# Spreading the gates into G in one pipeline of fixed order, with a tile of scores beside every 16 tokens and 52 tiles ahead

## The chip, the core and the metric

The kernel runs on one core of a Trainium2 chip. The metric is the device time in microseconds (us); the kernel before takes 2368.05 us, the median of 3 runs. TensorE (PE) does the matrix products, VectorE (DVE) and ScalarE (ACT) the elementwise work, GpSimd (POOL) some elementwise work and the issue of indirect DMAs, SyncE (SP) the issue of all other DMAs.

## The reference, cut to what matters

The program is two transformer blocks. The change lies in the feed-forward of the first, a mixture of 16384 experts (`u` and `v` are [16384, 1024]) of which each of 512 tokens uses 16 for each of 8 heads:

```python
def block(xi):
    q = (xi @ w_q).reshape(n, 8, 2, 128)
    s = jnp.einsum('nhpc,hpkc->nhpk', q, sub_keys)
    ts, ti = lax.top_k(s, 16)
    cand_s = ts[:, :, 0, :, None] + ts[:, :, 1, None, :]       # 16 x 16 pairs
    cand_i = ti[:, :, 0, :, None] * 128 + ti[:, :, 1, None, :]
    best_s, best_p = lax.top_k(cand_s, 16)
    idx = jnp.take_along_axis(cand_i, best_p, axis=-1)
    gate = jax.nn.softmax(best_s, axis=-1)
    act = gelu(jnp.einsum('nd,nhkd->nhk', xi, u[idx]))
    return jnp.einsum('nhk,nhkd->nd', gate * act, v[idx])
```

## The kernel before

For the first 384 tokens the kernel computes every expert: G[expert, token] holds the gates, zero where an expert is not chosen, and the result is the sum over 128 tiles of 128 experts of v_tile^T (G * gelu(u_tile x)). For the last 128 tokens it gathers the 128 chosen rows of u and of v for each token.

Products are made in three passes (`mm3`, lines 220 to 223): high half by high half, and the two mixed ones. A tile of u (512 KB) is split on the chip: `wsplit` loads it (`uraw`), ACT makes the high half `uhi` (line 233), and VectorE or POOL makes the low half `ulo` (line 234). `prep_u(i)` does this for tile i; `upass(i)` makes its 24 matmuls of 384 columns into `pu` and its gelu `ge` on ACT (line 986). `prep_u` gives the low half to POOL for tiles 3 to 41 and to VectorE for the others.

The stage runs in this order:

- **Routing** (16 column tiles of w_q): PE makes queries and scores, VectorE the sorted choices. After each column tile, `ahead` computes one or two tiles of u x ahead of time, 24 in all; their gelus go to DRAM (`sd`).
- **Spread**: G for 384 tokens. `spread(nt)` takes 128 tokens. It transposes the two key numbers and the gates (line 1096), makes doubled copies (`tw`), and then for every 64 tokens the short one-hot rows `bh`, `eql`, `bl` (lines 1114 to 1120). For every 8 tokens VectorE makes three operands of 128 x 1024 in 16 bits: the one-hot `oa` (line 1125) and two products `ob` (line 1131). PE multiplies them, 16 matmuls of 128 columns for 8 tokens (line 1139), into two PSUM tiles `pq`, and ACT copies each of these to `gs` or `gk` (line 1140), from where 64 tokens at a time go to DRAM (`gd`). Every fourth group of 8 tokens `ahead(1)` adds a tile of u x, 12 in all; `ahead(NG)` then does the rest up to NG = 43. The order of all this on the engines is set by a scheduler with priorities and modelled times.
- **Loop** over 128 tiles of v. `prep_v(i)` loads a tile of v and of G (`gt`), gets the scores (`gl` from DRAM for i < NG, `ge` from `upass` otherwise), multiplies them with G on VectorE (lines 1185, 1186), and splits both (`vhi`, `vlo`, `ch`, `cl`); `vpass(i)` makes 18 matmuls of 512 columns into `po`. From tile 43 on, `upass(i + 1)` runs beside `vpass(i)`. VectorE's order is written out by hand.
- The loop also holds the 256 gathers (128 of u rows, then 128 of v rows; `gr`, three buffers, 512 KB each). POOL issues them (line 1206), VectorE consumes them in order (line 1211 for u, line 1220 for v), between the low half of a tile of u and the products with G. Their number in one turn of the loop follows from a cost of 2 for a turn with a tile of u and 0.5 for one without: with NG = 43 the total is 187.5, which makes 256 x 2 / 187.5 = 2.73 gathers in a turn with u, and 0.68 in one without.

Of the kernel before, what the change touches and what calls it, by code (L numbers as in the profile page):

```python
# [20 lines left out]
D = 1024  # L21
# [10 lines left out]
# the even tokens, and the odd ones  # L32
# [133 lines left out]
def _nabias(rpb):  # L166
    """[4 blocks, 8 heads, 128 queries (c, r), 256 keys (c, r)]: the bias, or NEG outside the window"""
# [14 lines left out]
def _sib():  # L182
    """pairs (j, i) whose blocks of s are siblings, s = 1..32"""
    j = np.arange(128)[:, None]
    i = np.arange(128)[None, :]
    return np.stack([(((j // s) ^ (i // s)) == 1).astype(np.float32) for s in (1, 2, 4, 8, 16, 32)], 1)


def program(tc, a, dbg=None):
# [54 lines left out]
    def rstd_of(pool, ps, n, feat, eps, tag="rs", bufs=1, b=None):  # L244
        """-2 feat / sqrt(ps / feat + eps), with one Newton step; the gains carry the factor -1 / (2 feat)"""
# [10 lines left out]
    def warm_rs(after):  # L256
        """the table of the norms, ahead of one"""
# [6 lines left out]
    # ---------------------------------------------------------------- first block, mixing  # L264
# [11 lines left out]
    NG = 43  # L276
    GT = 3
    GN = 3
    OAN = 8
    PQB = 6  # L280
    # the order of the first projection's parts; the last one runs after the others' pools are closed
# [20 lines left out]
    with ExitStack() as es:  # L302
# [10 lines left out]
        def ada_steps():  # L313
            """the conditioning columns: products of rows of the transposed weights with the vectors, and their sums"""
# [29 lines left out]
        def weights():  # L344
            """the next tile of weights; the ones after it are on their way"""
# [14 lines left out]
        # the norm's factor scales the products' columns; the operands hold the gains alone  # L360
# [26 lines left out]
        def rs_columns():  # L387
            """the factor of a token's row, for tiles that have the tokens on the partitions"""
# [14 lines left out]
        def rotate(raw, j):  # L403
            """rotary embedding of a projected tile"""
# [103 lines left out]
        for o in order[:NT]:  # L508
            if o == 'z':
                x0.close()  # L510
                zp = x0.enter_context(tc.tile_pool(name="z", bufs=1, reuse_waits="tile"))
                # lambda
# [8 lines left out]
                V.tensor_scalar(lam, lam, 0.8 - 0.6, -1.0, op0=OP.add, op1=OP.mult)   # -lambda  # L521
# [14 lines left out]
        # ------------------------------------------------ gated linear attention, both directions  # L536
# [12 lines left out]
        def gla_pair(hp):  # L549
# [9 lines left out]
            def diag(h):  # L559
                """the 128 x 128 blocks on the diagonal of A^T"""  # L560
# [79 lines left out]
            # the meta tokens: forward, from the end of their decay to the start of the sequence  # L640
# [42 lines left out]
    # ------------------------------------------------ conditioning of the second block  # L683
# [6 lines left out]
    scl = const.tile([128, 3, KT], F32, name="scl")   # norm gain * (1 + scale): latent 1, context, latent 2  # L690
# [48 lines left out]
        # ------------------------------------------------ differential attention  # L739
# [123 lines left out]
    def shifted(pool, src, n, sc_, sh, rs, hi, lo):  # L863
        """src * gain * rs + shift in two halves"""
# [21 lines left out]
    with ExitStack() as es:  # L886
# [5 lines left out]
        # the context: its norm now, its keys and values behind the output projection  # L892
# [54 lines left out]
    # ------------------------------------------------ experts: scores and routes  # L947
# [20 lines left out]
    # ------------------------------------------------ experts: every expert for the first 384 tokens  # L968
# [10 lines left out]
    def upass(i):  # L979
        wh, wl = us.pop(i)  # L980
        p = psU.tile([128, ND], F32, name="pu")
        for k in range(KT):
            w_ = (wh[:, k * 128:k * 128 + 128], wl[:, k * 128:k * 128 + 128])
            mm3(p, w_, (hn[0][:, k, :ND], hn[1][:, k, :ND]), k == 0, k == KT - 1)
        ge = up.tile([128, ND], F32, name="ge", bufs=4)
# [6 lines left out]
    with ExitStack() as es:  # L992
# [7 lines left out]
        def route(h):  # L1000
            """the 16 best pairs of a head, as two key numbers, for every token"""
            tf = wp.tile([128, 4, 2, 16], BF16, name="tf")
            V.tensor_copy(tf, ti[:, :, 2 * h:2 * h + 2])
            # a pair (a, b) of ranks can be among the best 16 only if (a + 1) (b + 1) <= 16
# [28 lines left out]
            for c in range(2):  # L1033
                # the best 8 have ranks below 8
# [35 lines left out]
        # gates: a softmax over the 16 of each head, the first of which is the largest  # L1070
# [6 lines left out]
    # the last 64 tokens' part stays on chip  # L1077
# [13 lines left out]
    def spread(nt):  # L1091
        """G[i2, i1, n], through DRAM: a sum of products of one-hot rows, the gates scaled and in two halves"""
# [4 lines left out]
        # i1 = 16 a + b; every number twice, so that the last step of an operand is one element  # L1097
        iu = rp.tile([128, 2, 128], U32, name="iu", bufs=1)
        V.tensor_copy(iu[:, 0], p[:, 0:128])
        V.tensor_scalar(iu[:, 1], iu[:, 0], 15, None, op0=OP.bitwise_and)  # L1100
        tw = [rp.tile([128, 128, 2], F16, name=f"tw{j}", bufs=1) for j in range(5)]
        d2 = [128, 128, 2]
        V.tensor_copy(tw[1], iu[:, 1, :, None].to_broadcast(d2))
        V.tensor_tensor(tw[0], p[:, 0:128, None].to_broadcast(d2), tw[1], op=OP.subtract)
        S.copy(tw[2], p[:, 128:256, None].to_broadcast(d2))
        S.mul(tw[3], p[:, 256:384, None].to_broadcast(d2), GS)
        V.scalar_tensor_tensor(tw[4], p[:, 256:384, None].to_broadcast(d2), GS, tw[3], op0=OP.mult, op1=OP.subtract)
        for n0 in range(0, 128, 64):
            tb = nt * 2 + n0 // 64
            gs = gk if tb % 2 else rp.tile([128, 128, 64], F32, name="gs")  # L1110
            ns = slice(n0, n0 + 64)
            bh = rp.tile([128, 64, 8, 2], F16, name="bh", bufs=1)
            eq = rp.tile([128, 64, 16], F16, name="eql", bufs=1)
            V.tensor_tensor(bh, iotah[:, None].to_broadcast([128, 64, 8, 2]),
                            tw[0][:, ns, None, :].to_broadcast([128, 64, 8, 2]), op=OP.is_equal)
            V.tensor_tensor(pairs(eq), pairs(iota16[:, None, 0:16]).to_broadcast([128, 64, 8, 2]),
                            tw[1][:, ns, None, :].to_broadcast([128, 64, 8, 2]), op=OP.is_equal)
            bl = rp.tile([128, 2, 64, 16], F16, name="bl", bufs=1)
# [680 lines left out]
```

## Time and profile before

| | |
|---|---|
| time, median of 3 runs (lowest to highest) | 2368.05 us (2366.97 to 2370.98) |
| the profiled execution: span from first to last instruction | 2382.4 us |
| PE, weight loads, VectorE, ACT, POOL busy in it | 95%, 80%, 72%, 42%, 30% |
| start of the spread, start of the loop's first matmul | about 638 us, 805.86 us |
| turn of the loop without u, with u | about 4.07 us, 8.35 us |

The page of the profile gives no other time of the profiled execution than its span; it is 14.35 us (0.6%) above the median of the runs without a profile, so differences in it are carried over to the median as they are. Matmuls are pipelined, and the record of one reaches into the next, so the rate of the PE is read from the distances of starts or the number of matmuls in a stretch, not from busy time. [...]

### The profile page before, as it was taken

The numbers are of one execution on the slowest core, as the hardware profiler recorded it, in microseconds if no ns is written. First come the engines' busy times: TensorE is split into PE (matmuls) and PEld (weight loads), VectorE is DVE, ScalarE is ACT, GpSimd is POOL, SyncE is SP. The second block draws the span as 40 slices with busy tenths as digits, with TensorE's granted clock in tenths as the row PEclk, the third lists the DMA queues.
The fourth block names the chain that finished last, engine by engine and source line by source line (L and its number), as shares of the span: only waits on it lengthen the run. The fifth ranks groups of instructions, "written<-read, shape, count | busy, mean of one in ns | idle before, by whom it ended". The sixth has DMA issues, their size and how long they took to land.

```text
span 2382.4 us, 30940 instructions
## 1 busy us (share of the span) xinstructions
PE 2258.9 (95%) x11457; PEld 1895.9 (80%) x11457; DVE 1722.6 (72%) x3152; ACT 993.4 (42%) x1439; POOL 703.3 (30%) x428
## 2 busy tenths in 40 slices
PE   7999898999888999999999999999998999999997
PEld 6876466899767888899999987889877677788885
DVE  8997776799988677777777767778679565433334
ACT  5337774333277533333333323333443654322322
POOL 2132213344333311234343444443463023000001
PEclk9999998999989999999999999999999999999999
DMA  7760022533255899889999888889521221322320
GB/s 252 254 212 9 1 102 76 183 124 102 98 194 229 323 307 305 292 312 327 313 315 326 293 279 286 293 296 339 173 98 53 69 93 50 136 98 89 106 89 36
DMA packets 153831, 448.69 MB, mean 188 GB/s; under 512 B 14768, under 2 KB 58160, under 8 KB 151888
## 3 DMA queue, kind: packets, MB, share of 16 engines
q1 hardware_dynamic: 116768, 312.36, 37.5%
q0 software_dynamic: 36912, 134.37, 16.4%
q8 instruction: 89, 1.46, 0.2%
q14 instruction: 62, 0.51, 0.1%
HBM read 415.15 MB, written 31.52 MB: 187 GB/s over the span
## 4 chain that ended last, share of the span: by engine, by line
PE 73%; DVE 12%; DMA 6%; issue 4%; ACT 3%; POOL 2%; DVEq 0%; POOLq 0%; SPq 0%; ACTq 0%
PE pu L223 6%; PE pu L221 6%; PE po L221 6%; PE po L222 6%; PE po L223 6%; PE pu L222 6%; DMA gr<-in_v,idx 5%; PE psB L221 3%; PE psB L222 2%; PE psB L223 2%; PE pm L222 2%; PE pm L223 2%; PE pm L221 2%; PE pa L221 2%; PE pa L222 2%
## 5 line engine op out<-in xcount | busy, mean ns | idle before, releaser
L223 PE MATMUL pu<-hn,ulo 128*128 128x384 f32 x1024 | 353.4, 345 | 12.5 <-POOL ulo L234 12.5
L221 PE MATMUL pu<-hn,uhi 128*128 128x384 f32 x1024 | 354.2, 346 | 0.8 <-ACT uhi L233 0.8
L222 PE MATMUL pu<-hn,uhi 128*128 128x384 f32 x1024 | 351.7, 343 | 0.0
L221 PE MATMUL po<-vhi,ch 128*128 128x512 f32 x768 | 302.8, 394 | 9.4 <-ACT ch L1187 9.4
L222 PE MATMUL po<-vlo,ch 128*128 128x512 f32 x768 | 302.3, 394 | 0.4
L223 PE MATMUL po<-vhi,cl 128*128 128x512 f32 x768 | 300.8, 392 | 0.0
L234 POOL TENSOR_TENSOR wlo<-wraw,whi 128x1024 fp32r<-128x1024 f32 x57 | 144.5, 2540 | 398.0 <-ACT whi L233 328.2
L233 ACT CAST whi<-wraw 128x1024 fp32r<-128x1024 f32 x109 | 114.0, 1049 | 345.0 <-PE pm L222 126.7
L1206 POOL DMA_INDIRECT gr<-in_u,idx x128 | 148.2, 1158 | 344.8 <-DVE aact L1211 324.8
L1206 POOL DMA_INDIRECT gr<-in_v,idx x128 | 177.4, 1386 | 231.9 <-DVE acc L1220 190.7
L233 ACT CAST uhi<-uraw 128x1024 fp32r<-128x1024 f32 x129 | 135.6, 1051 | 248.9 <-PE pu L222 215.0
L1220 DVE SCALAR_TENSOR_TENSOR acc<-gr,aact,acc 128x1024 f32<-128x1024 f32 x126 | 159.0, 1280 | 87.7 <-DMA gr<-in_v,idx 87.1
L223 PEld LDWEIGHTS pu<-hn,ulo 128*128 128x128 f32 x1024 | 194.9, 190 | 13.4 <-POOL ulo L234 13.1
L221 PEld LDWEIGHTS pu<-hn,uhi 128*128 128x128 f32 x1024 | 194.9, 190 | 4.9 <-ACT uhi L233 0.9
L222 PEld LDWEIGHTS pu<-hn,uhi 128*128 128x128 f32 x1024 | 194.5, 190 | 4.1
L1176 ACT CAST vhi<-vraw 128x1024 fp32r<-128x1024 f32 x128 | 134.4, 1050 | 149.5 <-PE po L223 92.0
L1188 DVE TENSOR_TENSOR vlo<-vraw,vhi 128x1024 fp32r<-128x1024 f32 x128 | 156.1, 1220 | 42.9 <-ACT vhi L1176 42.9
L234 DVE TENSOR_TENSOR wlo<-wraw,whi 128x1024 fp32r<-128x1024 f32 x52 | 63.5, 1222 | 160.7 <-ACT whi L233 160.6
L221 PEld LDWEIGHTS po<-vhi,ch 128*128 128x128 f32 x768 | 144.5, 188 | 40.9 <-ACT ch L1187 13.3
L1211 DVE CUSTOM_DVE_ANT_0 gr<-gr,hnat 128x1024 f32<-128x1024 f32 x128 | 153.7, 1220 | 27.8 <-DMA gr<-in_u,idx 27.5
L223 PEld LDWEIGHTS po<-vhi,cl 128*128 128x128 f32 x768 | 144.4, 188 | 35.1 <-DVE cl L1189 4.0
L234 POOL TENSOR_TENSOR ulo<-uraw,uhi 128x1024 fp32r<-128x1024 f32 x39 | 123.2, 3163 | 157.8 <-ACT uhi L233 149.0
(567 smaller groups left out, 5106.1 us busy)
## 6 DMA issues: line engine op xcount, KB each, us to landing
uraw<-in_ut SPq DMA_DIRECT2D x129, 512.0 KB, 5.1
vraw<-in_v SPq DMA_DIRECT2D x128, 512.0 KB, 5.6
aw<-in_ada SPq DMA_DIRECT2D x48, 512.0 KB, 4.9
gt<-gd SPq DMA_DIRECT2D x42, 480.0 KB, 7.3
wraw<-in_m SPq DMA_DIRECT2D x32, 512.0 KB, 3.7
xraw<-in_m SPq DMA_DIRECT2D x32, 512.0 KB, 4.2
gd<-gs SPq DMA_DIRECT2D x6, 2048.0 KB, 9.8
sd<-ge SPq DMA_DIRECT2D x43, 192.0 KB, 2.1
```

What stands on the lines that cost most here:

```text
L221: PE.matmul(out, lhs[0], rhs[0], start=first, stop=False)
L222: PE.matmul(out, lhs[0], rhs[1], start=False, stop=False)
L223: PE.matmul(out, lhs[1], rhs[0], start=False, stop=last)
L233: S.copy(hi, raw)
L234: eng.tensor_sub(lo, raw, hi.bitcast(F32))
L1176: S.copy(wh, raw)
L1188: V.tensor_sub(wl, raw, wh.bitcast(F32))
L1206: G.indirect_dma_start(r, None, src, bass.IndirectOffsetOnAxis(ap=idx[:, j:j + 1], axis=0))
L1211: V.tensor_tensor_reduce(out=r, in0=r, in1=hnat, scale=1.0, scalar=0.0, op0=OP.mult, op1=OP.add, accum_out=aact[:, j:j + 1])
L1220: V.scalar_tensor_tensor(A, r, aact[:, j:j + 1], A, op0=OP.mult, op1=OP.add)
```

## The change

- The spread is written as one pipeline of 48 steps of 8 tokens. VectorE, ACT and PE follow the order in which it is written (`manual_schedule`).
- Every two steps (16 tokens) one tile of u x runs: 24 tiles, 26 to 49. Within a step PE does 8 of the spread's matmuls, then 6 of the tile's, and both again.
- VectorE makes the operands of step s + 2 while PE works on step s; `oa` and `ob` have three buffers in place of two. The short rows are made for 32 tokens at a time, not 64.
- The low halves of these 24 tiles are made on VectorE; POOL makes them for tiles 3 to 26.
- The last tokens' index list (`idx`) is made at step 3, not ahead of the spread.
- NG is 52 in place of 43: 24 tiles in routing as before, 2 between routing and the spread, 24 in the spread, 2 behind it. The loop then has 52 turns without u, and the total of its costs is 174: 2.94 gathers in a turn with u, 0.74 in one without.

```diff
-    NG = 43
+    NR = 26
+    NG = 52
...
-            us[i] = wsplit(up, a['ut'][i], bufs=2, tag="u", eng=G if 3 <= i < NG - 1 else V)
+            us[i] = wsplit(up, a['ut'][i], bufs=2, tag="u", eng=G if 3 <= i <= NR else V)
+
+    def prep_u_hi(i):
+        raw = up.tile([128, 1024], F32, name="uraw", bufs=3)
+        nc.sync.dma_start(raw, a['ut'][i])
+        us[i] = [up.tile([128, 1024], F32R, name=t, bufs=2) for t in ("uhi", "ulo")] + [raw]
+        S.copy(us[i][0], raw)
+
+    def prep_u_lo(i):
+        hi, lo, raw = us[i]
+        V.tensor_sub(lo, raw, hi.bitcast(F32))
...
+    CH = 32
...
+    def spread_rows(t):
+        tw = tws[t // 128]
+        ns = slice(t % 128, t % 128 + CH)
...
+    def spread_ops(s):
+        if s * 8 % CH == 0:
+            spread_rows(s * 8)
...
+        oa = rp.tile([128, 8, 128], F16, name="oa", bufs=3)
...
+        ob = rp.tile([128, 2, 8, 128], F16, name="ob", bufs=3)
...
-    for nt in range(3):
-        for b, _ in enumerate(spread(nt)):
-            if b % 8 in (1, 5):
-                ahead(1)
...
-    ahead(NG)
+    NS = 48
+    with tc.manual_schedule(engines={e.engine for e in (nc.vector, nc.scalar, nc.tensor)}):
+        i0 = ges["next"]
+        for i in range(i0, NR):
+            prep_u(i + 1)
+            upass(i)
+        spread_pre(0)
+        spread_ops(0)
+        spread_ops(1)
+        ti = NR
+        held = None
+        for s in range(NS):
+            if s % 2 == 0:
+                if held is not None:
+                    ugelu(*held)
+                prep_u_hi(ti + 1)
+                held = ti, psU.tile([128, ND], F32, name="pu")
+            if s + 2 < NS:
+                spread_ops(s + 2)
+            if s % 2 == 0:
+                prep_u_lo(ti + 1)
+            if s % 16 == 12 and s < 32:
+                spread_pre(s // 16 + 1)
+            for q0 in (0, 4):
+                spread_mm(s, q0)
+                k0 = (s % 2) * 4 + q0 // 2
+                umm(*held, range(k0, k0 + 2))
+            if s % 2:
+                ti += 1
...
+        ugelu(*held)
+        for i in range(ti, NG):
+            prep_u(i + 1)
+            upass(i)
```

On VectorE in the spread, before: the end of one 8-token group, the short rows of the next 64 tokens, and the next `oa`.

```order
L1131 TENSOR_TENSOR ob<-bh,bl 128x1024 x2
L1116 TENSOR_TENSOR eql<-iota_5646,tw_5658 128x1024
L1114 TENSOR_TENSOR bh<-iotah,tw_5657 128x1024
L1120 TENSOR_TENSOR bl<-eql,tw_5660 128x1024
L1120 TENSOR_TENSOR bl<-eql,tw_5661 128x1024
L1125 TENSOR_TENSOR oa<-iota_5646,tw_5659 128x1024
```

The same place of VectorE in the changed kernel, where lines 1142 to 1162 make the same operands and line 971 the low half of a tile of u.

```order
L1142 TENSOR_TENSOR bh<-iotah,tw_6302 128x512
L1143 TENSOR_TENSOR eql<-iota_5646,tw_6303 128x512
L1146 TENSOR_TENSOR bl<-eql,tw_6305 128x512
L1146 TENSOR_TENSOR bl<-eql,tw_6306 128x512
L1157 TENSOR_TENSOR oa<-iota_5646,tw_6304 128x1024
L1162 TENSOR_TENSOR ob<-bh,bl 128x1024 x2
L971 TENSOR_TENSOR ulo<-uraw,uhi 128x1024
```

The short rows are half as long, and a low half stands in VectorE's row after every second group.

On POOL from the end of routing to the end of the gathers, before (`cw0lo` belongs to the second block).

```order
L234 TENSOR_TENSOR ulo<-uraw,uhi 128x1024 x20
L1206 DMA gr<-in_u,idx 128x1024 x2
L234 TENSOR_TENSOR ulo<-uraw,uhi 128x1024
L1206 DMA gr<-in_u,idx 128x1024 x126
L1206 DMA gr<-in_v,idx 128x1024 x128
```

The same place of POOL in the changed kernel.

```order
L234 TENSOR_TENSOR wlo<-wraw,whi 128x1024
L234 TENSOR_TENSOR ulo<-uraw,uhi 128x1024 x6
L1274 DMA gr<-in_u,idx 128x1024 x128
L1274 DMA gr<-in_v,idx 128x1024 x128
L234 TENSOR_TENSOR cw0lo<-uraw,cw0hi 128x1024
```

Of 21 low halves 6 are left on POOL, all ahead of the spread, and its next work is the gathers.

On VectorE in the loop, in the part with the gathers of v, before: the sums of gathered rows (`acc`) in one turn, then the products with G and the splits, and the next turn's low half.

```order
L234 TENSOR_TENSOR ulo<-uraw,uhi 128x1024
L1220 SCALAR_TENSOR_TENSOR acc_7622<-gr,aact,acc_7622 128x1024
L1220 SCALAR_TENSOR_TENSOR acc_7621<-gr,aact,acc_7621 128x1024
L1185 TENSOR_TENSOR ge<-ge,gt 128x320
L1186 TENSOR_TENSOR ge<-ge,gk 128x64
L1188 TENSOR_TENSOR vlo<-vraw,vhi 128x1024
L1189 TENSOR_TENSOR cl<-ge,ch 128x384
```

The same part of VectorE's row in the changed kernel.

```order
L234 TENSOR_TENSOR ulo<-uraw,uhi 128x1024
L1288 SCALAR_TENSOR_TENSOR acc_7973<-gr,aact,acc_7973 128x1024
L1288 SCALAR_TENSOR_TENSOR acc_7972<-gr,aact,acc_7972 128x1024
L1288 SCALAR_TENSOR_TENSOR acc_7973<-gr,aact,acc_7973 128x1024
L1253 TENSOR_TENSOR ge<-ge,gt 128x320
L1254 TENSOR_TENSOR ge<-ge,gk 128x64
L1256 TENSOR_TENSOR vlo<-vraw,vhi 128x1024
L1257 TENSOR_TENSOR cl<-ge,ch 128x384
```

Before, a turn with two gathers follows every two or three turns with three; now turns with three follow each other up to 21 times.

## Rows read from the trace of the kernel before

**Rows 1.** Windows by stage: length, engines' busy time (instructions), granted clock, DMA share, GB/s.

```profile
638.00:806.00 168.00, 140.27 (x1199) 122.63 (x1200) 130.29 (x201) 117.08 (x139) 67.66 (x18) 0.89 0.57 216
806.00:977.00 171.00, 171.00 (x755) 141.28 (x754) 127.27 (x225) 63.08 (x86) 25.56 (x27) 1.00 0.93 313
977.00:1290.00 313.00, 313.00 (x1575) 285.48 (x1575) 244.37 (x390) 112.40 (x150) 122.68 (x101) 1.00 0.90 315
1290.00:1700.00 410.00, 400.14 (x1955) 354.56 (x1955) 310.62 (x362) 134.52 (x186) 174.55 (x126) 1.00 0.85 297
```

**Rows 2.** Waits of PE from 420 to 810 us: total us, times, longest.

```profile
PE pq L1139 <- DVE ob L1131: 15.0, 5, 4.8
PE pu L223 <- POOL ulo L234: 12.5, 3, 4.7
```

**Rows 3.** Waits of VectorE: 977 to 1290 us (first two), 1290 to 1700 us.

```profile
DVE ge L1185 <- ACT ge L986: 40.2, 29, 3.4
DVE gr L1211 <- DMA gr<-in_u,idx: 27.5, 24, 3.4
DVE acc L1220 <- DMA gr<-in_v,idx: 87.1, 48, 7.0
DVE ge L1185 <- ACT ge L986: 10.7, 9, 2.5
```

**Rows 4.** The sums of v rows on VectorE: count, shortest/median/longest ns, first and last start.

```profile
L1220 DVE SCALAR_TENSOR_TENSOR acc<-gr,aact,acc x126: 1273/1280/1306, 1295.8 to 1695.5; 128x1024 f32<-128x1024 f32 x126
```

**Rows 5.** Gathers of v rows on POOL, 1290 to 1700 us: busy, mean ns | idle; landing.

```profile
L1206 POOL DMA_INDIRECT gr<-in_v,idx x126 | 175.6, 1393 | 230.6 <-DVE acc L1220 190.7 <-DMA gr<-in_v,idx 20.8 <-issue 14.3
DMA to landing us min/median/max: 4.0/6.1/11.6
```

**Rows 6.** Timeline of PE in the spread and at both its ends: start, length, what.

```profile
653.33 0.28 PE L1139 MATMUL pq<-ob,oa 128*128 128x128 f16 x2 [3.15 <-DVE ob L1131]
...
674.03 0.95 PE L1139 MATMUL pq<-ob,oa 128*128 128x128 f16 x14
674.79 0.42 PE L223 MATMUL pu<-hn,ulo 128*128 128x384 f32 x1
675.05 0.34 PE L221 MATMUL pu<-hn,uhi 128*128 128x384 f32 x1
...
805.86 0.39 PE L221 MATMUL po<-vhi,ch 128*128 128x512 f32 x1
```

**Rows 7.** Timeline of VectorE: end of routing, and groups of the spread.

```profile
640.78 0.67 DVE L1076 TENSOR_TENSOR gate<-gate,gz 128x512 f32<-128x512 f32 x1
...
669.58 0.68 DVE L1116 TENSOR_TENSOR eql<-iota,tw 128x1024 f16<-128x1024 f16 x1
...
671.98 0.68 DVE L1125 TENSOR_TENSOR oa<-iota,tw 128x1024 f16<-128x1024 f16 x1
...
673.79 0.68 DVE L1125 TENSOR_TENSOR oa<-iota,tw 128x1024 f16<-128x1024 f16 x1
```

**Rows 8.** Timeline of ACT in the spread.

```profile
674.63 3.84 ACT L1140 ACTIVATE gk<-pq 128x512 f32<-128x512 f32 x4 [0.93 <-PE pq L1139]
678.24 1.08 ACT L233 CAST uhi<-uraw 128x1024 fp32r<-128x1024 f32 x1
...
680.90 0.56 ACT L986 ACTIVATE ge<-pu 128x384 f32<-128x384 f32 x1
```

**Rows 9.** Low halves on POOL in the spread, and on VectorE in the loop.

```profile
671.53 14.09 POOL L234 TENSOR_TENSOR ulo<-uraw,uhi 128x1024 fp32r<-128x1024 f32 x2 [7.84 <-ACT uhi L233]
L234 DVE TENSOR_TENSOR ulo<-uraw,uhi 128x1024 fp32r<-128x1024 f32 x86 | 104.6, 1216 | 0.0
```

**Rows 10.** A window of 25 us in the loop, columns as in rows 1.

```profile
1625.00:1650.00 25.00, 25.00 (x127) 22.80 (x126) 21.59 (x27) 8.87 (x13) 9.18 (x9) 1.00 0.94 344
```

**Rows 11.** Timeline of POOL: two issues of gathers, one behind the other.

```profile
1416.88 4.17 POOL L1206 DMA_INDIRECT gr<-in_v,idx  x1 [0.30 <-issue]
1421.35 0.94 POOL L1206 DMA_INDIRECT gr<-in_v,idx  x1 [0.31 <-issue]
```

More of the change, by code (lines that the diff above doesn't have):

```diff
@@ L979, in upass, with umm, ugelu @@
     def upass(i):
-        wh, wl = us.pop(i)
         p = psU.tile([128, ND], F32, name="pu")
-        for k in range(KT):
+        umm(i, p, range(KT))
+        ugelu(i, p)
+    def umm(i, p, ks):
+        wh, wl = us[i][:2]
+        for k in ks:
             w_ = (wh[:, k * 128:k * 128 + 128], wl[:, k * 128:k * 128 + 128])
             mm3(p, w_, (hn[0][:, k, :ND], hn[1][:, k, :ND]), k == 0, k == KT - 1)
+        if KT - 1 in ks:
+            us.pop(i)
+    def ugelu(i, p):
         ge = up.tile([128, ND], F32, name="ge", bufs=4)
@@ L1089, in pairs, with spread_pre @@
         return ap.rearrange("p n (a b) -> p n a b", b=2)
-    def spread(nt):
+    CH = 32
+    tws = {}
+    def spread_pre(nt):
         i1, i2, g = (t[:, nt].rearrange("p h k -> p (h k)") for t in (*ij, gate))
@@ L1098, in spread @@
         iu = rp.tile([128, 2, 128], U32, name="iu", bufs=1)
+        tw = [rp.tile([128, 128, 2], F16, name=f"tw{j}", bufs=2 if j == 2 else 1) for j in range(5)]
+        d2 = [128, 128, 2]
         V.tensor_copy(iu[:, 0], p[:, 0:128])
+        S.copy(tw[2], p[:, 128:256, None].to_broadcast(d2))
+        S.mul(tw[3], p[:, 256:384, None].to_broadcast(d2), GS)
         V.tensor_scalar(iu[:, 1], iu[:, 0], 15, None, op0=OP.bitwise_and)
-        tw = [rp.tile([128, 128, 2], F16, name=f"tw{j}", bufs=1) for j in range(5)]
@@ L1147, in program @@
-    for nt in range(3):
-        for b, _ in enumerate(spread(nt)):
-            if b % 8 in (1, 5):
-                ahead(1)
-    i1, i2, g = (t[:, 3].rearrange("p h k -> p (h k)") for t in (*ij, gate))
-    V.tensor_copy(gnat, g)
-    V.scalar_tensor_tensor(i1, i1, 128.0, i2, op0=OP.mult, op1=OP.add)
-    V.tensor_copy(idx, i1)
-    ahead(NG)
+        tws[nt] = tw
+    chunk, onehot, gsb = {}, {}, {}
+    def spread_rows(t):
+        tw = tws[t // 128]
+        ns = slice(t % 128, t % 128 + CH)
+        b4 = [128, CH, 8, 2]
+        bh = rp.tile([128, CH, 8, 2], F16, name="bh", bufs=1)
+        eq = rp.tile([128, CH, 16], F16, name="eql", bufs=1)
+        bl = rp.tile([128, 2, CH, 16], F16, name="bl", bufs=1)
+        V.tensor_tensor(bh, iotah[:, None].to_broadcast(b4), tw[0][:, ns, None, :].to_broadcast(b4), op=OP.is_equal)
+        V.tensor_tensor(pairs(eq), pairs(iota16[:, None, 0:16]).to_broadcast(b4), tw[1][:, ns, None, :].to_broadcast(b4),
+                        op=OP.is_equal)
+        for j in range(2):
+            V.tensor_tensor(pairs(bl[:, j]), pairs(eq), tw[3 + j][:, ns, None, :].to_broadcast(b4), op=OP.mult)
+        chunk[0] = bh, bl
@@ new lines, in spread_ops @@
+    def spread_ops(s):
+        if s * 8 % CH == 0:
+            spread_rows(s * 8)
+        bh, bl = chunk[0]
+        m, n1 = s * 8 % 128, s * 8 % CH
+        tw = tws[s // 16]
+        oa = rp.tile([128, 8, 128], F16, name="oa", bufs=3)
+        V.tensor_tensor(pairs(oa), pairs(iota16[:, None]).to_broadcast([128, 8, 64, 2]),
+                        tw[2][:, m:m + 8, None, :].to_broadcast([128, 8, 64, 2]), op=OP.is_equal)
+        ob = rp.tile([128, 2, 8, 128], F16, name="ob", bufs=3)
+        b4 = [128, 8, 8, 8, 2]
+        for j in range(2):
+            V.tensor_tensor(ob[:, j].rearrange("p n (a b c) -> p n a b c", a=8, c=2),
+                            bh[:, n1:n1 + 8, :, None].to_broadcast(b4),
+                            bl[:, j, n1:n1 + 8].rearrange("p n (b c) -> p n b c", c=2)[:, :, None].to_broadcast(b4),
+                            op=OP.mult)
+        onehot[s] = oa, ob
@@ new lines, in spread_mm @@
+    def spread_mm(s, q0):
+        oa, ob = onehot[s]
+        tb, n1 = s // 8, s % 8 * 8
+        if n1 + q0 == 0:
+            gsb[0] = gk if tb % 2 else rp.tile([128, 128, 64], F32, name="gs")
+        gs = gsb[0]
+        p = psR.tile([128, 512], F32, name="pq", bufs=PQB)
+        pv = p.rearrange("p (n a) -> p n a", n=4)
+        for q in range(4):
+            for j in range(2):
+                PE.matmul(pv[:, q], oa[:, q0 + q], ob[:, j, q0 + q], start=j == 0, stop=j == 1)
+        S.mul(gs[:, :, n1 + q0:n1 + q0 + 4].rearrange("p a n -> p n a"), pv, 1.0 / GS)
+        if n1 + q0 == 60 and tb < 5:
+            for q in range(0, 128, 64):
+                nc.sync.dma_start(gd[tb, :, q:q + 64], gs[:, q:q + 64])
@@ new lines, in program @@
+    NS = 48
[27 more added lines that the diff above has]
+                ti += 1
+            if s == 3:
+                i1, i2, g = (t[:, 3].rearrange("p h k -> p (h k)") for t in (*ij, gate))
+                V.tensor_copy(gnat, g)
+                V.scalar_tensor_tensor(i1, i1, 128.0, i2, op0=OP.mult, op1=OP.add)
+                V.tensor_copy(idx, i1)
+        ugelu(*held)
+        for i in range(ti, NG):
+            prep_u(i + 1)
+            upass(i)
```

41 lines of the change are left out of this document (removed).

## The prediction, before the run

> **What bounds the kernel now.** I read the page's shares of busy time first: PE is busy for 95% of the span and no other engine for more than 80%, so only what leaves PE idle, or slow, can be won. The windows by stage say where that is [rows 1]. Three stages hold the change. The spread takes 168 us, in which PE is busy for 140.27 and its clock averages 0.89. The loop's part without u and its part with gathers of u (to 1290 us) have PE busy throughout at clock 1.00. The part with gathers of v holds 1955 matmuls in 410 us. The stretch before it did 1575 in 313, so at that rate 1955 take 388.5 us: 21.5 us are lost there.
>
> The waits then say who makes PE late. In the spread it is VectorE's operand `ob` (15.0 us) and POOL's low halves (12.5 us) [rows 2]. In the loop VectorE stands between the gathers and the products with G, so I read its waits there [rows 3]. Beside gathers of u it waits mostly for ScalarE's gelu, which comes from PE's own last turn: VectorE is ahead of PE, and its 40.2 us are slack. Beside gathers of v it waits 87.1 us for gathered rows and only 10.7 for gelu: there the gathers set the pace.
>
> How fast can they go? The 126 sums of v rows start between 1295.8 and 1695.5, so one comes every 399.7/125 = 3.20 us; less the 10.7 us in which VectorE waited for gelu it is 3.11 [rows 3, 4]. The fixed number of buffers explains this. A gather's issue has a mean of 1.39 us, its landing a median of 6.1, and POOL waited 190.7 us for sums that free a buffer [rows 5]. With a sum of 1.28 us [rows 4] that is 8.77 us for one trip of a buffer, and with three buffers 2.92 us per gather, 3.11 with what else stands on VectorE between two sums.
>
> **The change part by part.** *Nine tiles move out of the loop.* A turn with u takes 313/(1575/42) = 8.35 us and one without 171/(755/18) = 4.08 [rows 1]. Each tile computed ahead turns one of the first kind into one of the second: 9 x (8.35 - 4.08) = 38.5 us off the loop, if the loop stays bound by PE.
>
> *They must fit into the spread.* Fourteen spread matmuls start within 674.79 - 674.03 = 0.76 us, 54 ns each, and the first u matmul behind them takes 0.26 us to the next start [rows 6]. One of 384 columns takes 4.28/24 = 0.178 us in the loop, by the difference of the turns. A step of the new order has 16 of the former and 12 of the latter, with two changes from the one to the other at 0.08 more: 16 x 0.054 + 12 x 0.178 + 0.17 = 3.17 us, 6.33 for a pair with its tile, and 48 x 3.17 = 152 us.
>
> *Do VectorE and ACT keep up with 6.33 us?* On VectorE a group of 8 tokens takes 673.79 - 671.98 = 1.81 us and the short rows of 64 tokens 671.98 - 669.58 = 2.40 [rows 7]; halves of these rows cost half and a little of fixed cost, some 0.7 us per pair. A low half takes 1.22 [rows 9]. With 0.2 for transposed numbers that is 2 x 1.81 + 0.7 + 1.22 + 0.2 = 5.7 us, 90% of the pair. ACT has four copies (678.24 - 674.63 = 3.61 us), a high half of 1.08 and a gelu of 0.56 [rows 8], 5.25 in all. Both fit, and operands two steps ahead leave 6 us of cover for a late one. If that cover is gone, each us by which a pair is longer costs 24.
>
> *Low halves leave POOL.* Two of them took 14.09 us beside VectorE's work, where VectorE needs 1.22 each [rows 9]. PE's 12.5 us of waits for them [rows 2] go; what is late next is `ob`, costed above. [...]
>
> *The start of the spread.* The gates are ready at 641.45 [rows 7]; before, the first spread matmul came at 653.33 [rows 6]. Now transposes, copies, four short rows and one group stand between: some 5.4 us by the durations above, so 646.8. `idx` moves behind it and saves a little of VectorE's row there; nobody waits for it before the loop. PE has little else to do then, because only tiles 24 and 25 come before. It is idle for some 12 us as before and then runs a while at the lower clock, for which I add 2.2 us. If the clock stayed at the 0.89 of this stage [rows 1] throughout, it would be 152 x 0.124 = 19.
>
> *The loop's start.* 646.8 + 2.2 + 152 + two tiles of 4.28 = 809.6, against 805.86 [rows 6]: +4. Behind the last pair the first products with G wait for a gelu that went to DRAM and back, with two tiles (8.6 us) as cover; I take **+5** and a range of +2 to +14 (the upper end with half of the clock's 19 us). At five places loads of u now stand behind three stores of scores on SP, each of which waits for its gelu. No row prices this; it is between nothing and 3 us each, taken as nothing, since a tile is loaded a pair ahead into three buffers.
>
> *Gathers per turn.* 52 turns without u instead of 43 raise the number in a turn with u from 2.73 to 2.94. PE's pace asks for one gather every 8.35/2.94 = 2.84 us, where it was 8.35/2.73 = 3.06. At 3.11 per gather of v, 125 intervals take 389 us while PE needs 355: 34 us lost, and the 4 us lost in this stage outside the sums (21.5 less 399.7 - 382.4) remain. The loss is 38 instead of 21.5, **+17**. Its bounds: at 3.20 it is 11 more, at 2.84 it is nothing and 21 are won. Bytes are no limit: 0.21 gathers of 512 KB more in a turn raise 315 GB/s [rows 1] by 13, and 344 were carried with PE at its full rate [rows 10]. In the part with gathers of u I charge nothing: VectorE waits for gelu 40.2 us in some 37 turns, 1.1 us each, and 0.21 more sums need 0.27.
>
> **Sum:** 2368 - 38.5 + 5 + 17 = **2352 us**, the median; the profiled execution, 14.35 us above it, would span about 2366.
>
> **The rivals.** *B, the gathers keep pace.* The long issues are what makes a trip long, and they lie beside certain stretches of VectorE's work; if the new order of turns falls more kindly, the loss stays at 21.5: 2368 - 38.5 + 5 = 2335 us, and 2314 if it vanishes. For it: the trip without long issues, 0.94 [rows 11] + 6.1 + 1.28 = 8.3 us, allows 2.8 per gather. Against it: turns with three gathers now follow each other up to 21 times, and the turns with two, in which a late gather was caught up, become rare. One issue took 4.17 us beside VectorE's products and splits, which have two inputs in SBUF [rows 11]. [...]
>
> *C, slower: the gathers bind beside u too.* VectorE's waits for u rows are already 27.5 us in 24 places [rows 3], each in a turn with three gathers. If three in every turn never catch up, 90 gathers of u run at 3.11 instead of 2.84, +25 us: 2352 + 25 = 2377. It decides when a u gather takes more than 2.84 + 16.5/90 = 3.02 us. Against it: the slack of 1.1 us per turn.
>
> *D, slower: the pipeline does not do what it says.* In a fixed order, a low half on VectorE waits for the high half on ACT, that stands behind copies which wait for PE. If the three take turns, a pair costs 7.3 us rather than 6.33, about what VectorE's 5.7 and a high half's 1.08 and a gelu's 0.56 would be in a row: +24, 2376 us. It decides from 6.33 + 16/24 = 7.0 us per pair. Against it: operands two steps ahead, six `pq`.
>
> **How the numbers follow.** The forecast has 0.55, B 0.20, C 0.14, D 0.11. The forecast's own range is 2340 to 2366, by the bounds of the start (-3 to +9) and of the gathers (-9 to +11) that are unlikely to meet. For 8 in 10 it is widened to B's 2335 and most of what lies below, and to the edge of C and D: **2326 to 2375**. What this kernel's measurement tells from no change is about 0.2%, 4.7 us. Faster than 2363.3: 0.47 of the forecast, all of B, 0.02 of the others, 0.69. Within: 0.08 and 0.07, 0.15. Slower than 2372.8: 0.16, from C and D.
>
> **What would show it.** Right, step by step: the loop's first matmul at 808 to 812 us of the new trace; pairs of spread steps every 6.3 us with the clock at 0.95 or more in the spread after its start; no waits of PE for low halves; turns with u still 8.35 us beside gathers of u; sums of v rows 3.1 us apart, and VectorE's waits for them above 87 us. Wrong: sums of v rows 2.85 apart (B), turns beside gathers of u of 9 us with waits for `gr` in place of gelu (C), a spread of 175 us with PE waiting for `ulo` or `ob` (D).

## The result, and the profile after

The changed kernel takes 2404.47 us (median, 2403.01 to 2412.78) beside 2369.52 us of the kernel before: a ratio of 1.0152, 95% interval 1.0114 to 1.019. It is 35 us slower, where 2352 was forecast, 16 us faster. The kernel before varies from execution to execution far more than the first three times showed (2358 to 2418 us in 48 more); why is part of what follows.

Windows by stage of the changed kernel (length; busy time of PE, its weight loads, VectorE, ACT, POOL, with instructions; granted clock as a share of full speed, DMA share, GB/s):

```profile
650.00:803.00 153.00, 152.69 (x1345) 137.73 (x1344) 134.65 (x223) 131.03 (x145) 4.42 (x3) 0.98 0.67 256
...
812.50:1022.00 209.50, 209.09 (x924) 172.97 (x923) 158.83 (x282) 77.02 (x106) 34.47 (x37) 1.00 0.94 318
1022.00:1300.00 278.00, 275.11 (x1367) 247.07 (x1366) 214.02 (x344) 94.32 (x130) 114.01 (x93) 1.00 0.89 313
1300.00:1720.00 420.00, 387.18 (x1795) 334.26 (x1796) 295.55 (x340) 120.34 (x170) 188.35 (x124) 0.96 0.80 279
```

Beside [rows 1]: in the spread PE is now busy throughout at clock 0.98 (before 140.27 of 168 us at 0.89). The turns without u are as before, 209.5/(924/18) = 4.08 us. The stretch with gathers of u holds 1367 matmuls in 278 us, which at 313/1575 = 0.199 us each take 271.7: 6 us lost, where nothing was. The stretch with gathers of v holds 1795, which take 356.7, in 420 us: **63 us lost**. PE is idle for 32.8 of these. By its mean in the stretch, 0.96 in place of 1.00, the clock takes some 17 us more (an estimate, 420 x 0.04). Behind a wait of 2.36 us, which ends at 1424.24, it is 0.55 from 1427 to 1430 us (0.50 in the first two of these, 0.65 in the third), with 1.00 up to 1426 and again from 1430. Matmuls of 512 columns, 0.23 us apart at clock 1.00, start up to 0.43 apart there: the eight from 1426.28 to 1429.68 take 3.40 us in place of 1.84. This late row thus cost PE 1.6 us more than the wait.

The spread in PE's row, its start, its rhythm, and the loop's first matmul:

```profile
644.75 0.48 PE L1119 MATMUL pq<-ident,gate 128*128 128x128 f32 x1
...
649.75 0.29 PE L1179 MATMUL pq<-ob,oa 128*128 128x128 f16 x1 [4.53 <-DVE ob L1162]
...
655.49 0.62 PE L1179 MATMUL pq<-ob,oa 128*128 128x128 f16 x8
...
657.06 0.62 PE L1179 MATMUL pq<-ob,oa 128*128 128x128 f16 x8
...
658.63 0.62 PE L1179 MATMUL pq<-ob,oa 128*128 128x128 f16 x8
...
812.48 0.39 PE L221 MATMUL po<-vhi,ch 128*128 128x512 f32 x1
```

Half a step takes 1.57 us, a pair 6.29. Of PE's waits of [rows 2], 15.0 us for `ob` and 12.5 for POOL's low halves, one row is left, 4.5 us of it before the first step:

```profile
PE pq L1179 <- DVE ob L1162: 4.8, 2, 4.5
```

VectorE's waits for gathered rows in the whole execution, to be read against [rows 3]:

```profile
DVE acc L1288 <- DMA gr<-in_v,idx: 124.0, 47, 6.7
...
DVE gr L1279 <- DMA gr<-in_u,idx: 43.4, 34, 3.3
```

The sums of v rows, against [rows 4], and the gathers of v on POOL, against [rows 5]:

```profile
L1288 DVE SCALAR_TENSOR_TENSOR acc<-gr,aact,acc x126: 1274/1281/1287, 1302.0 to 1718.6; 128x1024 f32<-128x1024 f32 x126
```

```profile
L1274 POOL DMA_INDIRECT gr<-in_v,idx x128 | 193.6, 1512 | 232.0 <-DVE acc L1288 195.6 <-issue 17.4 <-DMA gr<-in_v,idx 9.7
```

One sum comes every 416.6/125 = 3.33 us, and in this stretch VectorE waits for nothing else than rows. Eleven of the issues take over 3 us, ten of them 4.17; in the first profile of before there were seven. Here is one of the eleven, in VectorE's row and in POOL's:

```profile
1467.96 3.67 DVE L1288 SCALAR_TENSOR_TENSOR acc<-gr,aact,acc 128x1024 f32<-128x1024 f32 x3
1471.55 0.48 DVE L1253 TENSOR_TENSOR ge<-ge,gt 128x320 f32<-128x320 f32 x1
1471.95 0.21 DVE L1254 TENSOR_TENSOR ge<-ge,gk 128x64 f32<-128x64 f32 x1
1472.09 1.21 DVE L1256 TENSOR_TENSOR vlo<-vraw,vhi 128x1024 fp32r<-128x1024 f32 x1
1473.23 0.55 DVE L1257 TENSOR_TENSOR cl<-ge,ch 128x384 fp32r<-128x384 f32 x1
1473.69 1.21 DVE L234 TENSOR_TENSOR ulo<-uraw,uhi 128x1024 fp32r<-128x1024 f32 x1
1475.18 1.29 DVE L1288 SCALAR_TENSOR_TENSOR acc<-gr,aact,acc 128x1024 f32<-128x1024 f32 x1 [0.27 <-DMA gr<-in_v,idx]
1481.99 1.29 DVE L1288 SCALAR_TENSOR_TENSOR acc<-gr,aact,acc 128x1024 f32<-128x1024 f32 x1 [5.52 <-DMA gr<-in_v,idx]
```

```profile
1469.51 1.74 POOL L1274 DMA_INDIRECT gr<-in_v,idx  x1 [3.52 <-DVE acc L1288]
1471.55 4.17 POOL L1274 DMA_INDIRECT gr<-in_v,idx  x1 [0.30 <-issue]
1476.03 1.25 POOL L1274 DMA_INDIRECT gr<-in_v,idx  x1 [0.30 <-issue]
```

Because gathers were late, the sums and then the products stand in VectorE's row without a gap. The issue that begins together with the first product at 1471.55 ends at 1475.72, 0.8 us behind the low half's end at 1474.90: 3.35 us of the row and about the 0.94 of a short issue. Its row of v is the one that VectorE then waits 5.52 us for, and when that comes others are there too, so the next row has no gap either.

Two theories stood at the start. **T**: three buffers and the trip of a gather set the pace, so the number of gathers in a turn with u makes the loss. Rivals: the DMA engines are full (R1), or another part of the change slows the loop (R2).

### The profile page after: what moved, and what is told of

It is laid out like the page before. It is cut to its first block, busy times and chain, and to the rows that moved or that the text cites. A ratio compares the mean times of both kernels' runs of the same rounds, so it can differ in the third digit from the quotient of the medians.

```text
span 2401.0 us, 31002 instructions
## 1 busy us (share of the span) xinstructions
PE 2270.7 (95%) x11457; PEld 1894.2 (79%) x11457; DVE 1729.9 (72%) x3191; ACT 997.8 (42%) x1439; POOL 652.9 (27%) x413
## 4 chain that ended last, share of the span: by engine, by line
PE 53%; DMA 11%; issue 10%; DVE 7%; POOL 5%; ACT 1%; DVEq 0%; POOLq 0%; SPq 0%; ACTq 0%
DMA gr<-in_v,idx 10%; POOL gr L1274 4%; PE pu L221 4%; PE po L223 4%; PE po L221 4%; PE po L222 4%; PE pu L222 4%; PE pu L223 4%; PE pm L222 2%; PE pm L223 2%; PE pm L221 2%; PE pa L221 2%; PE pa L222 2%; PE pa L223 2%; PE pq L1179 2%
## 5 line engine op out<-in xcount | busy, mean ns | idle before, releaser
L221 PE MATMUL pu<-hn,uhi 128*128 128x384 f32 x1024 | 356.7, 348 | 2.0 <-DVE kc L928 2.0
L223 PE MATMUL pu<-hn,ulo 128*128 128x384 f32 x1024 | 346.5, 338 | 0.0
L221 PE MATMUL po<-vhi,ch 128*128 128x512 f32 x768 | 308.8, 402 | 34.8 <-ACT ch L1255 34.5
L222 PE MATMUL po<-vlo,ch 128*128 128x512 f32 x768 | 308.5, 402 | 0.9
L223 PE MATMUL po<-vhi,cl 128*128 128x512 f32 x768 | 307.4, 400 | 0.4 <-DVE cl L1257 0.4
L1274 POOL DMA_INDIRECT gr<-in_v,idx x128 | 193.6, 1512 | 232.0 <-DVE acc L1288 195.6
L1288 DVE SCALAR_TENSOR_TENSOR acc<-gr,aact,acc 128x1024 f32<-128x1024 f32 x126 | 158.5, 1281 | 124.4 <-DMA gr<-in_v,idx 124.0
L1255 ACT CAST ch<-ge 128x384 fp32r<-128x384 f32 x76 | 39.0, 514 | 366.3 <-DVE ge L1254 365.6
L1279 DVE CUSTOM_DVE_ANT_0 gr<-gr,hnat 128x1024 f32<-128x1024 f32 x128 | 154.4, 1221 | 43.6 <-DMA gr<-in_u,idx 43.4
L222 PEld LDWEIGHTS po<-vlo,ch 128*128 128x128 f32 x768 | 147.8, 192 | 38.0 <-DVE vlo L1256 9.1
```

Source lines behind the costliest of these rows:

```text
L221: PE.matmul(out, lhs[0], rhs[0], start=first, stop=False)
L222: PE.matmul(out, lhs[0], rhs[1], start=False, stop=False)
L223: PE.matmul(out, lhs[1], rhs[0], start=False, stop=last)
L1255: S.copy(ch, ge)
L1274: G.indirect_dma_start(r, None, src, bass.IndirectOffsetOnAxis(ap=idx[:, j:j + 1], axis=0))
L1279: V.tensor_tensor_reduce(out=r, in0=r, in1=hnat, scale=1.0, scalar=0.0, op0=OP.mult, op1=OP.add, accum_out=aact[:, j:j + 1])
```

## Experiments: the number of gathers, and the buffers

**Fewer gathers in a turn with u.** The changed kernel with only the cost of a turn without u changed:

```diff
-        WV = 0.5
+        WV = 0.76
```

> The changed kernel with the cost of a turn without u at 0.76 in place of 0.5: 2.73 gathers in a turn with u, as before the change, and 1.04 in one without (0.74). Theory T (three buffers and the length of a gather's trip set the pace, and the number of gathers in a turn with u makes the loss): the 420 us stretch with gathers of v, in which 63 us are lost, falls back to a loss of about 21 as before, the 6 us beside gathers of u vanish, so 2404 - 42 - 6 = 2356 us, with sums of v rows 3.1 to 3.2 us apart. Rival R1 (the DMA engines have no more room): the turns without u grow from 4.08 to about 4.3 us, 2368. Rival R2 (another part of the change slows the loop, such as the spread's new order or its memory): stays within 8 us of 2404.

2332.92 us (ratio to before 0.9878, 0.982 to 0.9937). Sums are 378.6/125 = 3.03 us apart, and VectorE's wait for rows of v fell from 124.0 to 17.4 us:

```profile
DVE gr L1279 <- DMA gr<-in_u,idx: 24.3, 23, 3.4
...
DVE acc L1288 <- DMA gr<-in_v,idx: 17.4, 22, 2.0
```

T's direction, but a bigger gain than it gave: with the same 2.73 gathers per turn the kernel before had waited 87.1 us. R2 is out: nothing but the number of gathers in a turn changed, and 71 us came back.

The same with `WV = 1.0`:

> The changed kernel with that cost at 1.0: 2.56 gathers in a turn with u, 1.28 in one without. T: a turn with u asks for one gather in 8.35/2.56 = 3.26 us, more than the 3.11 to 3.2 that the kernel before managed, so the loss with gathers of v nearly vanishes (0 to 8 of 63 us): 2335 to 2345 us. R1: the turns without u would carry 1.53 MB in 4.08 us, 375 GB/s, above all stretches seen, and grow to about 4.4 us each, 52 x 0.35 = 18 us of it given back, 2355. R2: within 8 us of 2404.

2331.62 us (0.9843, 0.9808 to 0.9878). The loop has no loss beside gathers of v (2084 matmuls in 414 us); the turns without u take 212.7/(927/18) = 4.13 us at 377 GB/s instead of 4.08. If that is R1's limit, which no run shows, it costs 3 us in all and not 18:

```profile
807.30:1020.00 212.70, 211.74 (x927) 173.44 (x928) 189.34 (x336) 81.99 (x106) 69.79 (x64) 1.00 1.01 377
1020.00:1236.00 216.00, 216.00 (x1086) 196.79 (x1085) 163.67 (x262) 77.22 (x104) 85.51 (x66) 1.00 0.91 310
1236.00:1650.00 414.00, 414.00 (x2084) 377.75 (x2083) 316.37 (x371) 147.29 (x197) 153.40 (x123) 1.00 0.87 298
```

**Four buffers**, with the number of gathers as in the change; the room comes from one accumulator in place of two:

```diff
-    acc = [vp.tile([128, D], F32, name=f"acc{j}") for j in range(2)]
+    acc = [vp.tile([128, D], F32, name=f"acc{j}") for j in range(1)]
...
-        r = vp.tile([128, D], F32, name="gr", bufs=3)
+        r = vp.tile([128, D], F32, name="gr", bufs=4)
...
```

> The changed kernel with four buffers for gathered rows in place of three; their room comes from one accumulator in place of two. T: a trip of 3 x 3.33 = 10 us over four buffers is 2.5 us per gather, below the 2.84 asked for, so the loss goes to about 0 to 10 of 63 and the time to 2335 to 2350 us. R1: trips get longer with more in flight, sums stay 3.2 to 3.3 us apart, 2390 to 2404. R2: within 8 us of 2404.

2330.74 us (0.9846, 0.9813 to 0.9878), with 2.94 gathers in every turn with u and no loss at all; VectorE's waits for rows are 2.3 and 1.2 us:

```profile
DVE acc L1288 <- DMA gr<-in_v,idx: 2.3, 3, 1.3
...
DVE gr L1279 <- DMA gr<-in_u,idx: 1.2, 3, 0.6
```

So with four buffers the DMA engines brought 2.94 rows per turn (beside gathers of v 318 GB/s, with 1846 matmuls in 367 us); with three, 63 us were lost at the same number. T stands, R1 falls.

**The number of tiles alone, in the kernel before:**

```diff
-    NG = 43
+    NG = 52
```

> The kernel before with 52 tiles ahead and nothing else of the change: its loop has 2.94 gathers in a turn with u. T: it loses the same 48 us more in the loop as the changed kernel, gains 38.5 there, and the nine tiles cost 9 x 4.28 = 38.5 less what falls into the idle time of PE in the spread (0 to 25): 2390 to 2416 us, sums of v rows 3.33 us apart. R2 (the loss comes from the new spread): sums 3.1 apart, loss 21, so 2345 to 2370 us.

2441.98 us (1.0311, 1.0225 to 1.0397), above T's 2390 to 2416. In the loop it shows the changed kernel's picture, sums 425.4/125 = 3.40 us apart and 133.1 us of waits:

```profile
DVE acc L1220 <- DMA gr<-in_v,idx: 133.1, 41, 7.1
...
DVE gr L1211 <- DMA gr<-in_u,idx: 52.8, 43, 3.0
```

The loss thus comes with the number of tiles, without the new spread. Its loop begins at 847.85 us, the changed kernel's at 812.48. The same tiles cost 35 us more in the old order of the spread: I had let up to 25 us of the nine tiles fall into PE's idle time there, and they added 36 to 42 (against 811.45 and 805.86 in two profiles of before).

## Experiments: the kernel before, and the long issues

**The kernel before with 1.0** as the cost of a turn without u:

> The kernel before with the cost of a turn without u at 1.0 in place of 0.5: 2.45 gathers in a turn with u, not 2.73, and 1.22 in one without. Theory T (the gathers per turn with u make the loss, before the change too): the 21.5 us lost beside gathers of v vanish but for 0 to 5, 2345 to 2353 us, with no issue above 2.5 us. Rival: that loss has another cause, within 6 us of 2368. It also gives what the spread's pipeline is worth without the gathers' loss: 2332 of the changed kernel with the same cost against this one.

2370.36 us (0.9984, 0.9952 to 1.0015): no gain, the time of the rival and not of T. Yet its trace has no loss beside gathers of v (2214 matmuls in 440 us, full rate). Both hold only if the 21.5 us of the first profile are not in the median. Between this kernel and the changed one at the same cost lie 2370.36 - 2331.62 = 38.7 us, what the nine tiles and the new spread bring when no gather is late.

**The kernel before, profiled once more:**

> The kernel before once more, with a second profile. Theory M (its time swings from execution to execution because the lateness of the gathers of v starts in some and not in others, and the first profile, 14.35 us above the median, was one in which it did): another loss than 21.5 us in the stretch with gathers of v, and a span that follows it, about 2361 plus the loss; the number of issues above 3 us differs from 7 with it. Rival: the surplus of the profiled execution is the same every time, a span of 2381 to 2384 and a loss of 20 to 23 us again.

A span of 2368.8 us and a time of 2370.94, against 2382.4 of the first profile. The stretch with gathers of v, and VectorE's and POOL's part in it:

```profile
1290.00:1690.00 400.00, 399.84 (x2007) 363.68 (x2006) 316.83 (x370) 141.77 (x191) 161.32 (x127) 1.00 0.88 309
```

```profile
DVE acc L1220 <- DMA gr<-in_v,idx: 32.6, 24, 7.0
```

```profile
L1206 POOL DMA_INDIRECT gr<-in_v,idx x128 | 162.4, 1269 | 231.0 <-DVE acc L1220 188.2 <-DMA gr<-in_v,idx 19.3 <-issue 18.9
```

2007 matmuls in 400 us, which would take 398.9: 1 us lost, where the first profile lost 21.5, with one issue above 3 us instead of seven. Theory M holds: the same kernel runs with and without late gathers, and the spans differ by 13.6 us: 20.5 less lost beside gathers of v, while its loop began 5.6 us later (811.45), which is most of what lies between 2368.8 and M's 2361 plus the loss. In the twelve profiled executions here of which both are known, the time is 1.7 to 2.7 us above the span (2370.94 and 2368.8, 2403.01 and 2401.0); the 14.35 us by which the first profile's span lay above the median was no cost of the profile, but a late execution.

**Gaps in VectorE's row.** Is a long issue a cause or a mark? The changed kernel with an operation of one column, without an input, in VectorE's row:

```diff
+    def gap():
+        if dm:
+            V.memset(dm[0], 0.0)
...
         V.tensor_mul(ge[:, 320:], ge[:, 320:], gk[:, i])
+        gap()
         S.copy(ch, ge)
         V.tensor_sub(wl, raw, wh.bitcast(F32))
+        gap()
         V.tensor_sub(cl, ge, ch.bitcast(F32))
+        gap()
...
             V.scalar_tensor_tensor(A, r, aact[:, j:j + 1], A, op0=OP.mult, op1=OP.add)
+            gap()
```

> The changed kernel with a fill of one column (128x1, no input) on VectorE behind every sum of a v row, behind the product with gk, and behind each of the two splits of prep_v: the row of operations with two inputs gets short gaps. Theory I (a gather's issue that meets VectorE's unbroken row waits for a gap; the late gather then makes the next row unbroken, so the lateness feeds itself): the 11 issues of 4.17 us among the gathers of v become none above 2.5 us, and of the 63 us lost beside gathers of v at least 35 come back: 2355 to 2370 us. Rival L (the long issues are only a mark of lateness; three buffers can't give a gather every 2.84 us): at least 50 us stay lost, 2390 to 2405 us, whether long issues are left or not.

2362.21 us (0.9921, 0.9874 to 0.9968): 42 us back by operations that compute nothing. No issue above 2 us is left (the longest takes 1.96), their mean is 1.23 us in place of 1.51, and sums are 377.1/125 = 3.02 us apart:

```profile
L1284 POOL DMA_INDIRECT gr<-in_v,idx x128 | 157.4, 1229 | 232.2 <-DVE dm L1237 201.7 <-issue 11.9 <-DMA gr<-in_v,idx 11.8
```

**Without the last of these four**, so that the sums stand in a row as they did and only the products are apart:

> The changed kernel with the one-column fills only behind the product with gk and behind the two splits of prep_v, none between the sums of v rows. Theory I, sharper: an issue of 4.17 us is one that began with the products and got through only behind the low half, 3.3 us of operations in one row and 0.94 of its own; gaps in that row alone suffice: no issue above 2.5 us, 2355 to 2368 us as with all the fills. Rival: it is the row of three sums that has to be broken; issues of 4 us remain and the time stays above 2390.

2366.61 us (0.9987, 0.9955 to 1.0019), again no issue above 2 us (the longest takes 1.87). The trace shows the same issue with the gap that was long without it. Ten of the eleven long issues of the changed kernel began within 0.01 us of the first product, right behind sums without a gap. Ten issues of this run do the same and take 1.43 us instead of 4.17; here is the first of them, whose product begins at 1310.77, in POOL's row:

```profile
1308.73 1.74 POOL L1284 DMA_INDIRECT gr<-in_v,idx  x1 [3.56 <-DVE acc L1298]
1310.78 1.43 POOL L1284 DMA_INDIRECT gr<-in_v,idx  x1 [0.31 <-issue]
```

So it is the row of products and splits that holds these issues up (4.17 us), and gaps in it free them (1.43). But not every issue that met the row waited for its end. In the changed kernel without gaps, those that begin 0.35 us behind the first product take 0.94 or 0.95 us (15 issues), and those that begin in the middle of the split `vlo` 1.36 or 1.37 (16 issues; the eleventh long one, of 3.12, began there too). One of each, where the first product begins at 1316.36 and `vlo` at 1323.82:

```profile
1316.72 0.95 POOL L1274 DMA_INDIRECT gr<-in_v,idx  x1 [1.96 <-DVE acc L1288]
...
1324.48 1.36 POOL L1274 DMA_INDIRECT gr<-in_v,idx  x1 [0.30 <-issue]
```

Which issue was held through the whole row was thus a matter of hundredths of a us (one that began at 1323.23, 0.02 us ahead of the product, took 0.94); why these and not the others is not shown. Theory I has its 38 to 42 us. The rest has the cause that rival L named, though it is less than L's 50: with every issue short, three buffers still leave 2362 - 2331 = 31 us to what four give.

## Experiments: the spread, and a faster version

**Low halves back on POOL**, in the changed kernel with cost 0.76:

```diff
     def prep_u_lo(i):
         hi, lo, raw = us[i]
-        V.tensor_sub(lo, raw, hi.bitcast(F32))
+        G.tensor_sub(lo, raw, hi.bitcast(F32))
```

> The changed kernel with 0.76 as the cost of a turn without u (2333 us by itself) and the low halves of the 24 tiles of the spread on POOL in place of VectorE. Theory S (VectorE's two-input operations and POOL's low half shut each other out, as in the 14.09 us that two of them took in the kernel before): a low half takes 5 us and more, VectorE is slowed by it, a pair of steps takes 7 to 8 us in place of 6.29, and the loop's first matmul comes 15 to 40 us later: 2348 to 2373 us. Rival: POOL fits into VectorE's gaps, as VectorE has 1.22 us less per pair to do; within 5 us of 2333.

2355.05 us (0.9931, 0.9882 to 0.998), 22 us slower by the medians than with them on VectorE, though the ranges overlap (2344.67 to 2393.87 and 2327.96 to 2349.37). The loop begins at 823.05 instead of 806.61, 16.4 us later. Of these, 4.5 us are no effect of the low halves: this execution was that much later already at the transposes of the gates (643.92 against 639.47), up to which the code is the same. From there the first spread matmul comes 2.2 us later and the 48 steps take 10 us more, 12 us in all. A pair still takes 6.29 us in most places, less than the 7 to 8 that I expected. A low half on POOL took 3.27 us in the mean (2.44 for the 24 ahead of the spread), not 5; PE waits for it only 0.8 us but 10.1 for `ob`, since VectorE's operations take longer in turn:

```profile
L1162 DVE TENSOR_TENSOR ob<-bh,bl 128x1024 f16<-128x1024 f16 x96 | 76.9, 839 | 0.0
L1157 DVE TENSOR_TENSOR oa<-iota,tw 128x1024 f16<-128x1024 f16 x48 | 38.4, 800 | 2.3 <-PE pq L1179 2.3
L1146 DVE TENSOR_TENSOR bl<-eql,tw 128x512 f16<-128x512 f16 x24 | 19.6, 857 | 0.4
```

The same with low halves on VectorE has 685, 686 and 422 ns in these rows. Theory S has its direction: beside each other both took longer. That the one stands still while the other works, no run shows. The two profiles differ by 2347.5 - 2326.2 = 21.3 us. The other 5 us lie behind the loop's first matmul, by the number of matmuls in its turns without u (4.21 us each against 4.07); beside gathers of v this profile loses nothing (1913 matmuls in 380 us). No trace shows what the slowest of its executions waited for.

**Five tiles ahead of the spread** in place of two, with four buffers and cost 1.0 (`NR = 29`, `NG = 55`):

> Four buffers for gathered rows with one accumulator, the cost of a turn without u at 1.0, and five tiles in place of two between routing and the spread (55 ahead in all). PE idles for some 10 us there while the gates and the first operands are made. If three tiles fit into that: 3 x 4.28 = 12.8 us less in the loop at an unchanged start of it, 2331 - 10 to 13 = 2318 to 2321 us. Rival: their low halves on POOL (2.4 us each at best) or their place in the fixed order delay the first spread matmul, 2326 to 2334.

2328.10 us (0.9811, 0.9733 to 0.9888): the rival. The three tiles stand ahead of the transposes in PE's fixed order and push these to 651 us, from 639 to 645 in the other profiles of the changed kernel; the loop begins at 818.99, so what its turns save is given up ahead of it.

**One tile behind the transposes** instead (`NR = 27`, `NG = 53`), with four buffers and cost 0.76:

```diff
-        for i in range(i0, NR):
+        for i in range(i0, NR - 1):
             prep_u(i + 1)
             upass(i)
         spread_pre(0)
         spread_ops(0)
         spread_ops(1)
+        prep_u(NR)
+        upass(NR - 1)
```

> Four buffers for gathered rows with one accumulator, the cost of a turn without u at 0.76, and one more tile ahead (53), whose products stand behind the first transposes in PE's row, in the 4.5 us in which PE waits for the first operands. Its low half is ready (636.5 us in the trace with cost 0.76) before the transposes (638.9 to 639.5). Expected: the first spread matmul where it was or up to 0.5 us later, a turn of 8.35 made one of 4.08 in the loop: 2331 - 4 = 2327 us, and with fewer bytes in the turns without u than at cost 1.0 another 1 to 3 off: 2323 to 2328. Rival: the tile's high half or low half delays the first copies or operands, no gain, 2330 to 2333.

**2324.61 us** (0.9811, 0.9736 to 0.9887), about 45 us faster than the kernel before and 80 than the change as it was. The tile takes the place of PE's wait of 4.5 us for the first operands:

```profile
640.54 0.48 PE L1119 MATMUL pq<-ident,gate 128*128 128x128 f32 x1
...
647.77 0.23 PE L1179 MATMUL pq<-ob,oa 128*128 128x128 f16 x1
...
648.37 0.55 PE L1179 MATMUL pq<-ob,oa 128*128 128x128 f16 x7 [0.37 <-DVE ob L1162]
```

## Why the prediction was wrong

**Nine tiles, -38.5 us: right.** With no late gather, new and old differ by 38.7 us (the kernel before and the changed one, both with cost 1.0), the start of the loop included. By their profiles 37.2 us of it lie behind the loop's first matmul (808.75 to 2368.0 against 807.30 to 2329.4).

**The pipeline of the spread: right.** A pair takes 6.29 us (6.33 forecast), nobody waits for low halves, and the clock is 0.98. Short rows of half the length cost somewhat more than half: 0.42 us, where whole ones took 0.68. The first spread matmul came at 649.75 rather than 646.8, since this execution reached the transposes of the gates at 644.75 (639.47 with cost 0.76, whose code up to there is the same); from there it took 5.0 us, where 5.4 were worked out from the gates on. The 2.2 us for the lower clock, for which the prediction names no row, came out near 2: from 650.35 to 655.49, at a clock of 0.56 (0.50 up to 654), 5.14 us went by for work of 3.09 at 1.57 us per half step. The loop began at 812.48, against 809.6 worked out and +5 taken, which is 810.9. Rival D was not seen. That low halves off POOL are worth something was right too, some 12 us at the loop's start.

**Gathers, +17: the step that failed, and in two places.** Against the second profile of before, the gathers cost 68 us more, 62 beside v and 6 beside u. First, the loss to start from. I took 21.5 us out of one profile, and carried its 14.35 us above the median over as a constant of the profile. The second profile of the same kernel shows 1 us of loss. The surplus should have been read as a sign that this execution held something the median did not. Measured from an undisturbed execution, the gathers of v could only get worse.

Second, the pace. The changed kernel's gathers of v came every 3.33 us, outside the bounds of 2.84 to 3.20 that I had given, and lost 63 us where 38 were worked out. I had taken a mean over turns with three gathers and turns with two, and held it for a property of the gathers. It depends on the turns. A turn with two lets a late gather catch up: in 8 of the 13 of them in the first profile of before, VectorE waits for no row of v, and five of these turns take only 5.67 to 6.01 us, where PE's pace is 8.35. (It does not keep issues short: four of the seven long issues of that profile, of 5.01 or 5.02 us, began in the second sum of such a turn.) With three in nearly every turn, up to 17 in a row by the code and not 21 as I had counted, lateness keeps itself up. Long issues rose from seven to eleven. The rows for this stood in the prediction, the 4.17 us of [rows 11] and the turns with two that become rare; I used them against rival B and did not follow them to their price.

**Beside gathers of u, nothing: wrong by 6 us.** VectorE's wait for them rose from 27.5 to 43.4 us. This is rival C's place, at a quarter of its price; C named the right mechanism, late gathers that never catch up, and the wrong stretch to charge for it.

The sum again, against the second profile of before: -38.5, +1 at the loop's start (812.48 against 811.45), +6 beside u and +62 beside v make +30.5; the spans differ by 2401.0 - 2368.8 = 32.2.

The trace alone does not show why a given execution of the kernel before falls into lateness and another does not. With cost 1.0 its ten executions lie within 8.2 us of each other, against 60 us for the kernel before, so most of what varies is in the gathers; what sets it off stays open.

## What to carry to other kernels

A profile is one execution: where its span lies off the median by more than the terms of the sum, look for the stretch that was unlucky in it before anything is carried over as constant. A rate read from a stretch with slack in every third turn is no bound for one without; count the buffers, multiply out the trip, and when the demand comes near, ask what a late transfer delays next. Moving work ahead of a loop also moves what was paced by the loop's turns: here a constant of the pace (0.5 to 0.76) was worth 71 us.

## What the runs showed of the hardware

An indirect gather's issue on GpSimd took 0.94 us at its shortest. In the changed kernel it took 4.17 us when it began within 0.01 us of the first of five VectorE operations of two inputs each, right behind sums without a gap (ten issues); begun 0.35 us behind the first product of such a row, it took 0.94 or 0.95 (15 issues). With operations of one column, without an input, behind the second, third and fourth of the five, the longest issue took 1.87 us. What in an issue was held up, no run tells.

The low halves on POOL took 3.27 us in the mean beside VectorE's work in the spread, and 2.44 ahead of it in the same execution; `ob` on VectorE took 839 ns beside them, in place of 685 without them.
